# Seven half products for two up-projection tiles in the MLPs of a four-layer encoder

## Chip, core and metric

The kernel runs on one core of a Trainium2 chip. The metric is device time in microseconds for one call, the median of several runs. Engines are called by their names in the profile: PE is TensorE (PEld its weight loads), DVE is VectorE, ACT is ScalarE, POOL is GpSimd, and SP is the engine whose queue issues the loads.

## What is computed

A hybrid encoder with 4 layers on 512 tokens of 1024 features, in fp32. Each layer has a mixer (retention in layers 0 and 3, a convolution in layer 1, gated linear attention in layer 2) and an MLP, both with a norm before and behind. The change concerns the MLPs, whose inner width is 4096:

```python
def sq_relu_mlp(u, w_up, w_down):
    return jnp.square(jax.nn.relu(u @ w_up)) @ w_down

for i in range(DEPTH):
    ...
    u = rmsnorm(h, norm_gains[i, 2])
    h = h + rmsnorm(sq_relu_mlp(u, mlp_w_up[i], mlp_w_down[i]), norm_gains[i, 3])
```

## The kernel before

Activations lie with features on partitions: `X` is 8 blocks of 128 features by 512 tokens. To keep fp32 accuracy every operand is cut into a high and a low part (`h` and `l` at the end of a name), and `mm3` (L394) makes each product of three matmuls, high x high, high x low and low x high (L397 to L399). A weight panel is 8 blocks of 128x128: what one output tile of 128 features by 512 tokens reads.

`Stream` (L94) brings the panels in. `prep` loads one into `wraw` (three buffers, L130), ScalarE writes the high part `whi` (L137), VectorE the low part `wlo` (L138). Both go into a ring of six slots (`ring`, L104), so a panel's cut waits until TensorE is done with the panel six places before. `next` keeps three panels ahead. `cut_early` (L147) does the same for panels of the convolution that follows layer 0, and writes both parts back to DRAM (L158), from where they are later loaded ready made.

`mlp` (L540 and on) has `FB` = 4 blocks. A block makes 8 up tiles (`proj`, 24 matmuls of 512 columns each) and then 8 down tiles, which read the block's 8 activations `act`. `up` evacuates a tile: relu times the token norm on VectorE (L561) into a scratch tile `tmp` (four of these), square on ScalarE (L562), then its high (L378) and low part (L385). `down` copies the result into `y` on ScalarE in block 0 (L246) and adds it on VectorE later (L251). Block 0 begins with `lead`, four tiles in halves while the norm is still computed; the last four down tiles of block 3 go through `trail`, in halves of 256 columns. `step`, called after tiles, cuts an early panel at every second call.

The order on TensorE is that of the program. On the other engines a scheduler orders the instructions when the kernel is built; at run time each engine takes them strictly in that order, each waiting for its semaphores.

`first_norm` (L434) loads the input and the first panels at the start, and adds the squares of the input for the first norm between them, in an order of its own.

## Time and profile before

| | us |
|---|---|
| median of 3 runs | 2757.65 (2756.64 to 2759.5) |
| profiled execution | 2759.13 |
| its span, first to last instruction | 2757.4 |
| TensorE busy | 2694.0 (98%) |
| VectorE busy | 1635.7 (59%) |
| ScalarE busy | 1191.1 (43%) |

The span is cut into stages that follow each other on TensorE. A busy share of the whole span says little of one stage, so the stretches of the MLP are read on their own. "Idle before" in a group is the time its engine stood still right ahead of these instructions. The granted clock (PEclk) is a share of full speed.

### The profile page before, as it was taken

Reading aid. Unit: us, or ns where it says so; the run is one execution under the profiler, and the core shown is the slowest. Engines: PE = TensorE matmul, PEld = TensorE weight load, DVE = VectorE, ACT = ScalarE, POOL = GpSimd, SP = SyncE. Lnnn points to the kernel's source line nnn. Section 1 sums busy time; section 2 is a strip of 40 time slices with the busy share of each in tenths; the row PEclk is TensorE's granted clock in tenths of the full one; section 3 lists DMA queues with packets and bytes.
Section 4 is the critical chain, followed back from the end, with each engine's and each line's share of the span. In section 5 each row is a group of like instructions: output and inputs, shape, how many; then the busy total and the mean of one; then the engine's idle time right before and its main releaser. Section 6 shows DMA issues by size and latency. Waiting matters only on the chain.

```text
span 2757.4 us, 33473 instructions
## 1 busy us (share of the span) xinstructions
PE 2694.0 (98%) x13312; PEld 2281.1 (83%) x13312; DVE 1635.7 (59%) x2517; ACT 1191.1 (43%) x1801; POOL 136.5 (5%) x133
## 2 busy tenths in 40 slices
PE   9999999999999699999999999999999999999998
PEld 7788888788898498888887888888888888988887
DVE  7755568445459974444587684444665555844444
ACT  5442445434337554332377554333444443543322
POOL 4000000000008500000000000000000000000000
PEclk9999999999999899999999999999999999999999
DMA  4222132666544013223122222223112212132221
GB/s 175 70 76 100 69 107 100 250 238 239 210 159 171 16 32 115 96 96 102 67 70 73 73 100 99 92 99 128 66 67 92 84 69 98 56 115 94 98 102 44
DMA packets 82669, 289.98 MB, mean 105 GB/s; under 512 B 9168, under 2 KB 11472, under 8 KB 82512
## 3 DMA queue, kind: packets, MB, share of 16 engines
q1 hardware_dynamic: 82368, 287.77, 29.8%
q8 instruction: 104, 1.70, 0.3%
q14 instruction: 53, 0.43, 0.1%
q10 hardware_dynamic: 144, 0.07, 0.0%
HBM read 260.02 MB, written 27.79 MB: 104 GB/s over the span
## 4 chain that ended last, share of the span: by engine, by line
PE 85%; DVE 7%; POOL 3%; ACT 2%; DMA 1%; issue 1%; SPq 0%; DVEq 0%; POOLq 0%; ACTq 0%
PE ps L398 28%; PE ps L399 28%; PE ps L397 28%; POOL y L918 2%; DMA wraw<-in_wst_dram 1%; DVE ps L933 1%; DVE wlo L138 1%; DVE acc L210 1%; DVE tmp L272 0%; PE st L218 0%; DVE h L275 0%; ACT whi L137 0%; POOL f L619 0%; DVE actl L385 0%; POOL k L618 0%
## 5 line engine op out<-in xcount | busy, mean ns | idle before, releaser
L137 ACT ACTIVATE whi<-wraw 128x1024 fp32r<-128x1024 f32 (+1 forms) x396 | 414.5, 1050 | 818.2 <-PE ps L398 730.9
L397 PE MATMUL ps<-xh,whi 128*128 128x512 f32 (+1 forms) x1984 | 736.9, 371 | 3.5 <-DVE tmp L561 2.5
L398 PE MATMUL ps<-xl,whi 128*128 128x512 f32 (+1 forms) x1984 | 734.1, 370 | 1.1 <-DVE xl L387 1.1
L399 PE MATMUL ps<-xh,wlo 128*128 128x512 f32 (+1 forms) x1984 | 733.9, 370 | 0.0
L138 DVE TENSOR_TENSOR wlo<-wraw,whi 128x1024 fp32r<-128x1024 f32 (+1 forms) x396 | 482.4, 1221 | 219.8 <-ACT whi L137 218.4
L397 PEld LDWEIGHTS ps<-xh,whi 128*128 128x128 f32 x1984 | 374.4, 189 | 68.0 <-issue 3.4
L398 PEld LDWEIGHTS ps<-xl,whi 128*128 128x128 f32 x1984 | 374.4, 189 | 65.6 <-DVE xl L387 1.5
L399 PEld LDWEIGHTS ps<-xh,wlo 128*128 128x128 f32 x1984 | 374.2, 189 | 63.7 <-DVE wlo L138 0.4
L398 PE MATMUL ps<-actl,whi 128*128 128x512 f32 x896 | 349.8, 390 | 1.4 <-DVE actl L385 1.4
L397 PE MATMUL ps<-acth,whi 128*128 128x512 f32 x896 | 348.8, 389 | 1.8 <-ACT acth L378 1.8
L399 PE MATMUL ps<-acth,wlo 128*128 128x512 f32 x896 | 348.6, 389 | 0.0
L251 DVE TENSOR_TENSOR y<-y,ps 128x512 f32<-128x512 f32 (+1 forms) x200 | 114.6, 578 | 315.9 <-PE ps L399 315.4
L561 DVE SCALAR_TENSOR_TENSOR tmp<-ps,rx 128x512 f32<-128x512 f32 x128 | 86.8, 689 | 228.0 <-PE ps L399 227.7
L398 PEld LDWEIGHTS ps<-actl,whi 128*128 128x128 f32 x896 | 168.2, 188 | 40.6 <-DVE actl L385 5.9
L397 PEld LDWEIGHTS ps<-acth,whi 128*128 128x128 f32 x896 | 168.2, 188 | 37.2 <-ACT acth L378 2.2
L399 PEld LDWEIGHTS ps<-acth,wlo 128*128 128x128 f32 x896 | 168.2, 188 | 34.2
L210 DVE TENSOR_TENSOR acc<-acc,sq 128x256 f32<-128x256 f32 (+1 forms) x245 | 116.4, 479 | 50.9 <-ACT sq L209 45.0
L397 PE MATMUL ps<-whi,xh 128*128 128x512 f32 (+1 forms) x384 | 138.3, 360 | 1.3 <-ACT xh L380 1.1
L399 PE MATMUL ps<-whi,xl 128*128 128x512 f32 (+1 forms) x384 | 137.2, 357 | 0.0
L398 PE MATMUL ps<-wlo,xh 128*128 128x512 f32 (+1 forms) x384 | 137.0, 357 | 0.1
L209 ACT ACTIVATE sq<-y 128x256 f32<-128x256 f32 (+1 forms) x105 | 47.0, 455 | 127.2 <-DVE y L251 105.1
L385 DVE TENSOR_TENSOR actl<-tmp,acth 128x512 fp32r<-128x512 f32 x128 | 87.5, 689 | 4.1 <-ACT acth L378 4.0
(323 smaller groups left out, 3839.5 us busy)
## 6 DMA issues: line engine op xcount, KB each, us to landing
wraw<-in_wst_dram SPq DMA_DIRECT2D x438, 512.0 KB, 3.5
cuth<-early SPq DMA_DIRECT2D x24, 512.0 KB, 2.6
cutl<-early SPq DMA_DIRECT2D x24, 512.0 KB, 3.0
whi<-cuth SPq DMA_DIRECT2D x20, 512.0 KB, 3.3
wlo<-cutl SPq DMA_DIRECT2D x20, 512.0 KB, 4.2
h<-in_xT_dram SPq DMA_DIRECT2D x8, 256.0 KB, 5.4
wraw<-in_wst_dram SPq DMA_DIRECT2D x8, 256.0 KB, 5.3
ww<-cuth SPq DMA_DIRECT2D x4, 512.0 KB, 7.1
```

The lines of the kernel that those rows point to most:

```text
L137: nc.scalar.activation(h, raw[:, c:d], AF.Copy)
L138: nc.vector.tensor_tensor(l, raw[:, c:d], h.bitcast(F32), ALU.subtract)
L209: nc.scalar.activation(t, src, AF.Square, scale=scale)
L210: nc.vector.tensor_tensor(acc, acc, t, ALU.add)
L251: self.K.nc.vector.tensor_tensor(y, y, ps[:, a:b], ALU.add)
L385: self.nc.vector.tensor_tensor(lo, src, hi, ALU.subtract)
L397: mm(out, lhsT=A[0], rhs=B[0], start=start, stop=False)
L398: mm(out, lhsT=A[0], rhs=B[1], start=False, stop=False)
L399: mm(out, lhsT=A[1], rhs=B[0], start=False, stop=stop)
L561: nc.vector.scalar_tensor_tensor(t[:, lo:hi], ps[:, lo:hi], 0.0, self.r[:, lo:hi], ALU.max, ALU.mult)
L918: nc.gpsimd.tensor_tensor(co[i], co[i], o, ALU.add)
L933: nc.vector.scalar_tensor_tensor(sums[i], x, w, sums[i], ALU.mult, ALU.add)
```

## The change

In blocks 1 to 3 of every MLP, two neighbouring up tiles are computed together by Strassen's scheme in its form with seven products. The 2x2 parts are: two output tiles, two halves of the features (4 blocks each), two halves of the tokens (256 columns). Each of the seven products has 4 blocks and 256 columns.

The weights need sums of the raw parts. `Stream.pair` loads two panels and makes four entries of the ring from them: the first panel as it is, a sum panel `t`, a second sum panel, and a half panel. The sums are four VectorE instructions of 128x512 per pair. The operand sums of the activations (`combos`, with tiles `wS`) are made once per MLP, between the down tiles 2 to 5 of block 0. `seven` runs the products into three PSUM tiles, two of which are accumulated on: ScalarE copies the state between products into scratch tiles `e1` and `e2`, VectorE joins them, and the joined tile goes to the old evacuation `up` from SBUF in place of PSUM. It keeps five entries ahead.

The first two down tiles of each block run side by side (`proj2`): blocks 0 to 5 of the one, of the other, then blocks 6 and 7 of both. Early panels are cut after each down tile alone, into slots of the ring, no longer after up tiles and into tiles of their own. The squares for the first norm aren't added in `first_norm` any more but by `norm_sums`, called from `norm`. The diff, cut to its core:

```diff
 class Stream:
...
-    def cut_early(self, i, pool):
+    def pair(self, i):
...
+        pool = self.pairs.pop(i)
+        self.loaded += 2
+        H = 4 * P
+        r1 = pool.tile([P, 8 * P], F32, name="raw1", tag="raw1", bufs=2)
+        r2 = K.wp.tile([P, 8 * P], F32, name="wraw", tag="wraw", bufs=3)
+        nc.sync.dma_start(r1, self.src[i])
+        nc.sync.dma_start(r2, self.src[i + 1])
+        tt = nc.vector.tensor_tensor
+
+        def cut(raw, w=8 * P):
+            hi, lo = self.ring()
+            self.ready.append(Panel(hi, lo))
+            nc.scalar.activation(hi[0][:, :w], raw[:, :w], AF.Copy)
+            tt(lo[0][:, :w], raw[:, :w], hi[0][:, :w].bitcast(F32), ALU.subtract)
+
+        def second():
+            t = K.wp.tile([P, 8 * P], F32, name="wraw", tag="wraw", bufs=3)
+            tt(t[:, :H], r2[:, :H], r1[:, :H], ALU.subtract)
+            tt(t[:, H:], t[:, :H], r2[:, H:], ALU.subtract)
+            cut(t)
+
+            tt(r1[:, :H], r2[:, H:], r2[:, :H], ALU.subtract)
+            tt(r2[:, :H], t[:, H:], r1[:, H:], ALU.add)
+
+        cut(r1)
+        self.steps = [second, lambda: cut(r2), lambda: cut(r1, H)]
+
+    def cut_early(self, i):
...
-        hi, lo = (pool.tile([P, 8 * P], F32R, name="early", tag="early", bufs=2) for _ in range(2))
+        hi, lo = (t[0] for t in self.ring())
...
 def first_norm(self):
...
-        self.hsum = Sums(self, D)
...
-                if k:
-                    for a, b in HALVES:
-                        self.hsum.add(self.h[k - 1][:, a:b], (a, b))
-            for a, b in HALVES:
-                self.hsum.add(self.h[KD - 1][:, a:b], (a, b))
...
+    def proj2(self, X, late=2):
+
+        ps = [self.ps() for _ in range(2)]
+        p = []
+        for ks in (range(KD - late), range(KD - late, KD)):
+            for i in range(2):
+                if len(p) < 2:
+                    p.append(self.W.next())
+                for k in ks:
+                    self.mm3(ps[i], p[i].blk(k), X[k], k == 0, k == KD - 1)
+        return ps
...
+    def combos(self, pool):
...
+        def make(k):
+            xa, xb, s = self.tmp(), self.tmp(), self.tmp()
+            nc.scalar.activation(xa, self.h[k], AF.Identity, scale=self.gain(*self.X_gain, k))
+            nc.scalar.activation(xb, self.h[4 + k], AF.Identity, scale=self.gain(*self.X_gain, 4 + k))
+            tt(s[:, :H], xa[:, H:], xb[:, H:], ALU.add)
+            tt(s[:, H:], xa[:, :H], s[:, :H], ALU.subtract)
+            tt(xb[:, :H], xb[:, :H], s[:, H:], ALU.add)
+            tt(xb[:, H:], xa[:, :H], xa[:, H:], ALU.subtract)
+            c = (k % 2 * T, (k % 2 + 1) * T)
+            self.split(S12[k // 2], s, c)
+            self.split(S34[k // 2], xb, c)
...
+    def seven(self, evac):
...
+        a, c, bd = self.ps(), self.ps(), self.ps()
+        e1, e2 = self.tmp(), self.tmp()
+        lo, hi = slice(0, H), slice(H, T)
+
+        def product(n, out, w, off, more=False):
+            S = self.S[n]
+            for k in range(4):
+                self.mm3(out, w.blk(off + k), S[k], k == 0 and not more, k == 3, more)
...
+        w = entry()
+        product(1, a[:, lo], w, 0)
+        copy(e1[:, lo], a[:, lo])
+        product(2, bd[:, lo], w, 4)
+        w = entry()
+        product(5, c[:, lo], w, 0)
+        copy(e2[:, hi], c[:, lo])
+        product(6, a[:, lo], w, 4, True)
+        copy(e2[:, lo], a[:, lo])
+        w = entry()
+        product(4, bd[:, hi], w, 0)
+        product(3, c[:, lo], w, 4, True)
+        nc.vector.tensor_tensor(e2[:, lo], c[:, lo], e2[:, lo], ALU.add)
+        w = entry()
+        product(7, a[:, lo], w, 0, True)
+        copy(e1[:, hi], a[:, lo])
+        nc.vector.tensor_tensor(e2[:, hi], e1[:, hi], e2[:, hi], ALU.add)
+        evac(1, e2)
+        nc.vector.tensor_tensor(e1, bd, e1, ALU.add)
+        evac(0, e1)
+        W.at += 2
...
 def mlp(self, close, early=()):
...
-            steps += 1
-            if early and steps % 2 == 0:
-                self.W.cut_early(early.pop(0), mp)
+            if early:
+                self.W.cut_early(early.pop(0))
...
+                if b:
+                    for n in range(0, KD, 2):
+                        self.seven(lambda i, t: up(n + i, t, (0, T), t))
+                    n0 = KD
                 for n in range(n0, KD):
                     ps = self.proj()
                     self.when(lambda n=n, ps=ps: up(n, ps, (0, T)))
-                    step()
...
+                for n, ps in enumerate(self.proj2(act)):
+                    complete(n, ps)
+                for n in range(2, n1):
+                    complete(n, self.proj(act))
+                    if b == 0 and n < 6:
+                        make(n - 2)
```

**VectorE in an up-projection** (block 1 of layer 1; `tmp` scratch, `rx` the token norm). Before, an evacuation, a panel's low part, a low part of the activation, in turn:

```order
L561 SCALAR_TENSOR_TENSOR tmp_9482<-ps_9457,rx_8993 128x512
L138 TENSOR_TENSOR wlo_9561<-wraw_9559,whi_9560 128x1024
L385 TENSOR_TENSOR actl_9368<-tmp_9482,acth_9367 128x512
L561 SCALAR_TENSOR_TENSOR tmp_9518<-ps_9493,rx_8993 128x512
L138 TENSOR_TENSOR wlo_9597<-wraw_9595,whi_9596 128x1024
L385 TENSOR_TENSOR actl_9370<-tmp_9518,acth_9369 128x512
```

Now, from the join in the second pair (L657) to the cut of the last entry of the fourth (L176); L184 and L185 are sums of raw weights, L661 and L663 joins:

```order
L657 TENSOR_TENSOR tmp_10331<-ps_10328,tmp_10331 128x256
L176 TENSOR_TENSOR wlo_10430<-raw1_10425,whi_10429 128x1024
L427 TENSOR_TENSOR actl_10171<-tmp_10189,acth_10170 128x512
L176 TENSOR_TENSOR wlo_10465<-wraw_10461,whi_10464 128x1024
L184 TENSOR_TENSOR raw1_10425<-wraw_10426 128x512
L661 TENSOR_TENSOR tmp_10331<-tmp_10330,tmp_10331 128x256
L185 TENSOR_TENSOR wraw_10426<-wraw_10461,raw1_10425 128x512
L690 SCALAR_TENSOR_TENSOR tmp_10331<-tmp_10331,rx_9745 128x512
L663 TENSOR_TENSOR tmp_10330<-ps_10329,tmp_10330 128x512
L176 TENSOR_TENSOR wlo_10496<-wraw_10426,whi_10495 128x1024
L690 SCALAR_TENSOR_TENSOR tmp_10330<-tmp_10330,rx_9745 128x512
L176 TENSOR_TENSOR wlo_10526<-raw1_10425,whi_10525 128x512
```

Three instructions for a tile have become twelve for a pair, without those of the raw sums that stand further ahead.

**SP's queue in layer 0's down-projections** (`cuth`, `cutl` the DRAM copies of an early panel's parts; `wraw` loads by L130/L139 are panels, by L152/L195 early ones). Before, block 1:

```order
L130 DMA wraw_4637<-in_wst_dram 128x1024
L152 DMA wraw_4673<-in_wst_dram 128x1024
L158 DMA cuth137_4679<-early_4675 128x1024
L158 DMA cutl137_4680<-early_4676 128x1024
L130 DMA wraw_4683<-in_wst_dram 128x1024
L130 DMA wraw_4715<-in_wst_dram 128x1024
```

Now, block 0:

```order
L139 DMA wraw_4165<-in_wst_dram 128x1024
L195 DMA wraw_4198<-in_wst_dram 128x1024
L201 DMA cuth130_4148<-whi_4144 128x1024
L201 DMA cutl130_4149<-wlo_4145 128x1024
L139 DMA wraw_4221<-in_wst_dram 128x1024
L195 DMA wraw_4254<-in_wst_dram 128x1024
L201 DMA cuth131_4204<-whi_4200 128x1024
L201 DMA cutl131_4205<-wlo_4201 128x1024
```

Two panels were loaded for each early one; now each panel's load is followed by an early one with its two writes.

**VectorE at the start** (`acc` the sum of squares, `sq` its low part for the norm's matmul, which TensorE waits for). Before:

```order
L210 TENSOR_TENSOR acc<-acc,sq 128x256 x2
L138 TENSOR_TENSOR wlo<-wraw,whi 128x1024
L603 TENSOR_TENSOR alo<-ang,ahi 128x512
L758 TENSOR_SCALAR nlb<-lg 128x4
L764 TENSOR_SCALAR E<-dist,lg 128x896
L138 TENSOR_TENSOR wlo<-wraw,whi 128x1024
L385 TENSOR_TENSOR sq<-acc,sq 128x512
L765 SCALAR_TENSOR_TENSOR E<-dist,nlb,E 128x896
L138 TENSOR_TENSOR wlo<-wraw,whi 128x1024 x3
```

Now:

```order
L252 TENSOR_TENSOR acc<-acc,sq 128x256
L905 SCALAR_TENSOR_TENSOR E<-dist,nlb,E 128x896
L147 TENSOR_TENSOR wlo<-wraw,whi 128x1024
L252 TENSOR_TENSOR acc<-acc,sq 128x256
L147 TENSOR_TENSOR wlo<-wraw,whi 128x1024
L252 TENSOR_TENSOR acc<-acc,sq 128x256
L147 TENSOR_TENSOR wlo<-wraw,whi 128x1024
L252 TENSOR_TENSOR acc<-acc,sq 128x256
L427 TENSOR_TENSOR sq<-acc,sq 128x512
L147 TENSOR_TENSOR wlo<-wraw,whi 128x1024
```

The additions and `sq` have moved behind the fifth full panel; they stood behind the third.

## Rows read from the trace of the kernel before

**Rows 1.** The page, part 1: busy us (share of the span) x instructions

```profile
PE 2694.0 (98%) x13312; PEld 2281.1 (83%) x13312; DVE 1635.7 (59%) x2517; ACT 1191.1 (43%) x1801; POOL 136.5 (5%) x133
```

**Rows 2.** The waits, TensorE: line, releaser: us in total, times, longest us

```profile
PE ps L218 <- DVE acc L212: 16.3, 1, 16.3
...
PE ps L397 <- ACT acth L378: 1.8, 1, 1.8
PE ps L398 <- DVE actl L385: 1.4, 5, 0.4
```

**Rows 3.** The groups by form, TensorE: busy us, mean ns | idle, releaser

```profile
L397 PE MATMUL ps<-xh,whi 128*128 128x512 f32 x1616 | 631.6, 391 | 2.5 <-DVE tmp L561 2.5
...
L397 PE MATMUL ps<-xh,whi 128*128 128x256 f32 x368 | 105.3, 286 | 0.9 <-ACT xh L380 0.9
```

**Rows 4.** The timeline, TensorE, an up-projection and a trail: start us, us, instruction

```profile
537.44 0.39 PE L399 MATMUL ps<-xh,wlo 128*128 128x512 f32 x1
...
542.88 0.39 PE L399 MATMUL ps<-xh,wlo 128*128 128x512 f32 x1
...
772.38 0.28 PE L398 MATMUL ps<-actl,ww 128*128 128x256 f32 x1
...
779.34 0.28 PE L399 MATMUL ps<-acth,ww 128*128 128x256 f32 x1
```

**Rows 5.** The windows, ups, downs: us, busy PE, PEld, DVE, ACT, POOL; PEclk, DMA share, GB/s

```profile
539.00:582.00 43.00, 43.00 (x191) 35.60 (x190) 24.45 (x28) 21.00 (x29) 0.00 (x0) 1.00 0.66 240
582.00:625.50 43.50, 43.50 (x194) 36.02 (x193) 19.84 (x20) 12.27 (x13) 0.00 (x0) 1.00 0.67 241
```

**Rows 6.** The groups by form, VectorE

```profile
L138 DVE TENSOR_TENSOR wlo<-wraw,whi 128x1024 fp32r<-128x1024 f32 x388 | 476.9, 1232 | 219.0 <-ACT whi L137 217.6
L385 DVE TENSOR_TENSOR actl<-tmp,acth 128x512 fp32r<-128x512 f32 x128 | 87.5, 689 | 4.1 <-ACT acth L378 4.0
...
L251 DVE TENSOR_TENSOR y<-y,ps 128x512 f32<-128x512 f32 x120 | 82.1, 686 | 279.5 <-PE ps L399 279.4
...
L275 DVE TENSOR_TENSOR h<-h,tmp 128x256 f32<-128x256 f32 x128 | 53.2, 417 | 0.0
...
L138 DVE TENSOR_TENSOR wlo<-wraw,whi 128x512 fp32r<-128x512 f32 x8 | 5.5, 684 | 0.8 <-ACT whi L137 0.8
```

**Rows 7.** The timeline, VectorE, the first MLP: full stretches

```profile
477.77 2.48 DVE L561 SCALAR_TENSOR_TENSOR tmp<-ps,rx 128x512 f32<-128x512 f32 x4
...
664.93 1.23 DVE L155 TENSOR_TENSOR early<-wraw,early 128x1024 fp32r<-128x1024 f32 x1 [0.57 <-ACT early L154]
666.07 1.22 DVE L138 TENSOR_TENSOR wlo<-wraw,whi 128x1024 fp32r<-128x1024 f32 x1
```

**Rows 8.** The groups by form, ScalarE

```profile
L137 ACT ACTIVATE whi<-wraw 128x1024 fp32r<-128x1024 f32 x388 | 409.5, 1059 | 817.3 <-PE ps L398 730.9 <-DMA wraw<-in_wst_dram 31.8 <-PE ps L399 29.7
L378 ACT ACTIVATE acth<-tmp 128x512 fp32r<-128x512 f32 x128 | 79.6, 629 | 3.1
...
L380 ACT ACTIVATE vh<-ps,rcol 128x256 fp32r<-128x256 f32 x12 | 4.9, 470 | 6.9 <-PE ps L399 6.2 <-DVE rcol L1072 0.6
```

**Rows 9.** The timelines, TensorE and ScalarE, first down tile of layer 0

```profile
493.53 0.50 PE L397 MATMUL ps<-acth,whi 128*128 128x512 f32 x1 [1.78 <-ACT acth L378]
...
491.24 1.06 ACT L154 ACTIVATE early<-wraw 128x1024 fp32r<-128x1024 f32 x1 [1.17 <-DMA wraw<-in_wst_dram]
```

**Rows 10.** The windows, layer 0, stretches of 2 us in the downs, columns as in rows 5

```profile
590.00:592.00 2.00, 2.00 (x10) 1.66 (x9) 1.16 (x2) 0.00 (x0) 0.00 (x0) 1.00 1.05 406
592.00:594.00 2.00, 2.00 (x11) 1.65 (x10) 0.87 (x2) 1.06 (x1) 0.00 (x0) 1.00 1.00 311
```

**Rows 11.** The timelines at the start, TensorE, VectorE and ScalarE

```profile
31.66 0.62 PE L228 MATMUL st<-sq,onesr 128*128 128x512 f32 x2
...
27.47 0.68 DVE L385 TENSOR_TENSOR sq<-acc,sq 128x512 fp32r<-128x512 f32 x1
...
29.10 1.06 ACT L137 ACTIVATE whi<-wraw 128x1024 fp32r<-128x1024 f32 x1 [1.28 <-DMA wraw<-in_wst_dram]
```

More of the change, by code (lines that the diff above doesn't have):

```diff
@@ L114, in prep @@
         i = self.loaded
+        if i in self.pairs:
+            self.pair(i)
+            return []
         self.loaded += 1
@@ L161, in next @@
         ahead = self.ahead if ahead is None else ahead
-        while len(self.ready) < 1 + ahead and self.loaded < self.n:
-            self.prep()
+        self.fill(1 + ahead)
         self.at += 1
@@ L172, in fill @@
     def fill(self, n):
-        while len(self.ready) < n and self.loaded < self.n:
+        while len(self.ready) < n and (self.steps or self.loaded < self.n):
             self.prep()
@@ L537, in trail, with part @@
             self.after(5.0 if c[1] == T else 2.5, lambda c=c: close.half(c))
+    def combos(self, pool):
+        nc = self.nc
+        tt = nc.vector.tensor_tensor
+        H = T // 2
+        new = lambda: [pool.tile([P, 8 * P], F32R, name="wS", tag="w", bufs=8) for _ in range(2)]
+        S12, S34 = [new(), new()], [new(), new()]
+        def make(k):
[9 more added lines that the diff above has]
+            self.split(S34[k // 2], xb, c)
+        def part(S, which):
+            out = []
+            for k in range(4):
+                a = k % 2 * T + which * H
+                out.append(self.cut(S[k // 2], (a, a + H)))
+            return out
+        low, high = (0, H), (H, T)
+        self.S = {
+            1: [self.cut(self.X[k], low) for k in range(4)],
+            2: [self.cut(self.X[4 + k], low) for k in range(4)],
+            4: [self.cut(self.X[4 + k], high) for k in range(4)],
+            5: part(S12, 0), 6: part(S12, 1), 3: part(S34, 0), 7: part(S34, 1),
+        }
+        return make
```

36 lines of the change are left out of this document (27 added, 9 removed).

## Prediction

> **What bounds the kernel now.** The busy times come first: TensorE is busy for 2694.0 of 2757.4 us [rows 1]. Then its waits: the longest is one of 16.3 us inside the convolution, and the waits for the MLP's activations come to 1.8 and 1.4 us over the whole run [rows 2]. In an up-projection and in the down-projection behind it TensorE has no gap, at full clock, while VectorE is busy for 24.45 of 43.00 us and 19.84 of 43.50, and ScalarE for 21.00 and 12.27 [rows 5]. So in the MLPs the end is set by how fast TensorE issues, and a matmul that is gone is time that is gone, as long as the two engines that prepare its operands keep up.
>
> The duration of one matmul, 391 ns for 512 columns and 286 ns for 256 [rows 3], isn't its price, since they overlap. The price is the distance between starts. In an up-projection 24 matmuls of 512 columns take 542.88 - 537.44 = 5.44 us, 226.7 ns each; in the last part of a down-projection, where each has 256 columns and a weight load of its own, 58 take 779.34 - 772.38 = 6.96 us, 120.0 ns each [rows 4]. Two halves thus cost 13 ns more than one whole.
>
> **Fewer columns on TensorE.** A pair of up-projection tiles had 2 x 8 x 3 = 48 matmuls of 512 columns: 48 x 226.7 ns = 10.88 us. It gets seven products of 4 blocks x 3 matmuls with 256 columns: 84 x 120.0 ns = 10.08 us. That is 0.80 us a pair. Blocks 1 to 3 of four MLPs have 4 pairs each, 48 pairs: **38.4 us less**, if nothing waits. One block's up-projection goes from 43.5 to 40.3 us. The price of a 256-column matmul is the trace's; the only thing it doesn't show is the order of operands, and that is the same (a fresh weight block for each matmul, whole blocks of 128 columns).
>
> The Trainium skill would give more: "TensorE: Matmul & The Clock Gate", section "Back-to-back issue gap", puts the distance at N/2.4 + 2.5 ns, 109.2 ns for 256 columns and 215.8 for 512. By it a pair would save 48 x 215.8 - 84 x 109.2 = 1186 ns, and 48 pairs an estimated 57 us. The trace doesn't agree, with 120.0 and 226.7 ns: a fixed part of 13 ns per matmul instead of 2.5, and that part is what more and shorter matmuls multiply.
>
> **What VectorE and ScalarE get for it.** Weights for a pair were two panels, each cut into a high part on ScalarE (1059 ns) and a low part on VectorE (1232 ns). Now they are three panels and a half, plus four additions of 128x512 between raw panels. Results are put together from four copies on ScalarE and three additions on VectorE (two of 256 columns, one of 512) before the two old evacuations. VectorE per pair, by durations [rows 6]: 3 x 1232 + 684 for the cuts, 4 x 684 for the raw sums (taken as the 512-wide subtraction), 2 x 417 + 686 for the joins, 2 x 689 + 2 x 689 for the evacuations: 11.4 us, after 5.2 before. Its instructions overlap, though: in a full stretch starts lie 1.14 us apart for 1024 columns, and four of 512 take 2.48 us, 0.62 each [rows 7]. With these, and 0.35 for 256, the sum is 3 x 1.14 + 10 x 0.62 + 2 x 0.35 = 10.3 us. TensorE's pair takes 10.08. ScalarE per pair: 3 x 1059 + half of that for the half panel, 4 x 470 (bounded by the 256-column read of PSUM), 4 x 629 [rows 8]: 8.1 us. So VectorE is just as long as TensorE within a pair, and is the engine to watch.
>
> It isn't over the edge for a block, since work slips out at both ends. Weights are prepared into a ring of six: all of the first pair (7.1 us by durations) and the first panel of the second (1.2) can be cut during the down-projection before, where VectorE is less than half busy [rows 5]. The last pair's evacuation, about 3.9 us, falls into the down-projection behind. Two down panels (2.5 us) come in. Four pairs by durations: 45.5 - 8.3 - 3.9 + 2.5 = 35.8 us, in 40.3. In the order of VectorE's instructions the 12 between the second pair's join and the third's come to 9.3 us by durations and 8.4 by starts, under 10.08; and the weights for the third and fourth pairs stand some 8 us ahead of the matmuls that read them.
>
> The tightest place is the scratch tiles: there are four, two to a pair, so the first copy of the fourth pair waits for the second pair's last evacuation. From the end of the third pair's sixth product VectorE has to do a join, a low part, two down panels, a join and a low part: 0.42 + 0.69 + 2 x 1.23 + 0.42 + 0.69 = 4.7 us, then ScalarE's copy 0.47. TensorE comes to the product that needs it four products later, 4 x 1.44 = 5.8 us. That leaves 0.6 us for four hand-offs between engines. Behind the waiting copy stand ScalarE's cuts of the next panels. No wait of this kind is in the trace; between 0 and 2.5 us a block, I take **0.3 us x 12 = +3.6 us**, near zero, since sums by starts leave over a microsecond.
>
> **Side by side.** The first two down tiles now leave blocks 6 and 7 of the activations for last, 36 matmuls (8.2 us) after the start instead of 18 (4.1). The fourth pair's evacuation ends later than a tile's did (two tiles at once: a copy 0.47, two joins 0.42 and 0.69, two evacuations 0.69 each, a square and a high part 0.63 each, a low part 0.69, 4.9 us behind the last product), so this is what covers it; without it each block would wait up to 1 us. Of the 3.2 us of waits for activations it can take between 0 and all. The longest stands in layer 0, where the activation is queued on ScalarE behind an early panel whose load landed late [rows 9]; those early panels leave the up-projections altogether. **-2.5 us.** The operand sums (four steps of four 256-wide additions and two low parts, 3.0 us of VectorE each) lie in the first block's down-projection, where that block's results are copied by ScalarE and VectorE has under half its time in use: nothing.
>
> **Layer 0's early panels.** 24 panels for the convolution are cut and written to DRAM; they were spread over every second tile of ups and downs, and now go one to each down tile of blocks 0 to 2. On SP's queue, per tile of 5.44 us, stand two reads of 512 KB and two writes of 512 KB: 2.1 MB, 386 GB/s. With all 16 engines busy the trace shows 406 GB/s in a stretch with such writes and 311 in the reads behind it [rows 10], so a tile needs about 1.05/0.311 + 1.05/0.406 = 6.0 us of transfers. Over eight tiles some 4 us are missing, three times. Panels are two tiles ahead, which hides that; what is left over shifts the start of the next up-projection's preparation, with VectorE nearly full. Between 0 and 12 us, **+3 us**, since the lead of the ring is longer than the lag. The early panels also take ring slots, so the first pair has only its first three entries ready there.
>
> **The start.** The sums of squares for the first norm were added in a fixed order among the first panels; now the scheduler puts them later. Their result was ready by 27.47 + 0.68 us, and TensorE read it at 31.66 [rows 11]. Now it stands on VectorE behind the fifth full panel, whose high part starts at 29.10: about 29.10 + 1.06 + 1.23, then an addition 0.42, a high part 0.63 and a low part 0.68 [rows 6, 8]: 33.1. **+1.5 us**, between 0 and 3.
>
> **Sum.** -38.4 + 3.6 - 2.5 + 3 + 1.5 = -32.8 us. The profiled execution took 2759.13 us with a span of 2757.4; the median of the runs is 2757.65, 1.5 lower. The change, summed on the profiled execution, is taken off the median: 2757.65 - 32.8 = 2724.9, say **2725 us**. With each of these costs at its best: 2757.65 - 38.4 - 3.2 = 2716.
>
> **Rivals.** (1) Hand-offs between ScalarE and VectorE cost more than 0.3 us a block. For it: VectorE has 10.3 to 11.4 us of work in a pair of 10.08, strictly in order, and each low part waits for a high part, which waits for a ring slot. Against: the 35.8 us of 40.3. At 1.5 to 2.3 us a block, 14 to 24 us more than I took: 2739 to 2749. (2) Layer 0's transfers aren't hidden: 12 us for the missing bandwidth, 9 more than I took, and as much again if the writes, which wait for both cuts, hold the reads behind them on SP: 2734 to 2746. (3) The other side: VectorE can't work ahead, because its queue stands at a join or a low part that waits for a ring slot until the up-projection begins. Then all 45.5 + 2.5 = 48.0 us lie in each of 12 up-projections of 43.5: +4.5 x 12 = 54 us, and with the other terms 2757.65 + 54 - 2.5 + 4.5 = 2814. It decides from 3.2 us of waits a block on, where the matmuls' gain is used up. (4) Waits of just that size: within 0.2% of before.
>
> **How the numbers follow.** A measurement of this kernel tells 0.2%, 5.5 us, from no change. My forecast, 2716 to 2735, has 0.62; rival 1 0.18; rival 2 beyond 2735 0.08; rival 4 0.05; rival 3 0.07. Faster: 0.62 + 0.18 + 0.08 = 0.88; same 0.05; slower 0.07. The range takes in the forecast and the first two rivals: 2714 to 2749.
>
> **What would show it.** In an up-projection after: starts of 256-column matmuls 0.12 us apart and pairs of 10.1 us; blocks of 40.3 to 40.8 us from the first product to the first down matmul; TensorE's waits for scratch copies and evacuations below 6 us in sum; VectorE busy for over 85% of the up-projections. Layer 0's downs should show transfers near full share and 43.5 us all the same. If starts are further apart than 0.12 us, the first term is wrong; if pairs are 10.5 us or longer with TensorE waiting on ScalarE's copies, rival 1 holds; if the waits are on low parts of weights, it is rival 3, or rival 2 where layer 0 alone has them.

## The result, and the profile after

The changed kernel takes **2717.48 us** (median of 4 runs, 2715.87 to 2719.07), the kernel before 2757.14 us beside it (4 runs, 2755.18 to 2759.5). The ratio is 0.9856, interval 0.9839 to 0.9873: 39.7 us faster. The prediction was 2725, range 2714 to 2749. Sign and size are right, but several terms of its sum are not, and one of them by far.

The profiled execution took 2716.43 us with a span of 2714.7, which is 42.7 us under the span of before. That is 3 us more than the medians say, because before's profiled run is late in its range and after's early. Part 1 of the page, and the waits of TensorE that are new or changed:

```profile
PE 2655.4 (98%) x15040; PEld 2332.1 (86%) x15040; DVE 1937.0 (71%) x3045; ACT 1363.1 (50%) x2153; POOL 135.2 (5%) x133
```

```profile
PE ps L440 <- DVE actl L427: 3.5, 8, 1.1
...
PE ps L439 <- ACT tmp L639: 1.3, 2, 1.0
...
PE st L270 <- ACT sq L420: 1.0, 1, 1.0
```

TensorE runs 1728 more matmuls in 39 us less busy time [rows 1]. The waits that the prediction feared (copies of the products, L639) occur twice in the whole run, and no low part of a pair's weights is waited for. The timeline of TensorE in an up-projection of layer 1, and three windows (columns as in rows 5): layer 0's block 1 ups, layer 1's block 1 ups, and the downs behind the latter. The last line is the kernel before, layer 1's block 1 ups:

```profile
1087.65 0.28 PE L439 MATMUL ps<-xh,whi 128*128 128x256 f32 x1
...
1088.85 0.28 PE L440 MATMUL ps<-xl,whi 128*128 128x256 f32 x1
```

```profile
521.90:564.00 42.10, 40.76 (x337) 40.34 (x336) 37.71 (x53) 28.00 (x46) 0.00 (x0) 1.00 0.56 186
1087.70:1128.00 40.30, 40.30 (x338) 40.30 (x337) 33.05 (x46) 27.08 (x44) 0.00 (x0) 1.00 0.43 136
1128.00:1171.50 43.50, 43.50 (x194) 36.01 (x193) 23.92 (x30) 10.87 (x13) 0.00 (x0) 1.00 0.22 69
```

```profile
1102.40:1145.80 43.40, 43.40 (x193) 35.95 (x192) 19.22 (x22) 17.00 (x23) 0.00 (x0) 1.00 0.28 97
```

Ten matmuls lie 1.20 us apart, the 0.120 us of [rows 4]. TensorE has no gap in 40.30 us, while VectorE is busy for 33.05 of them: 82%, in the same block before 44% (19.22 of 43.40; the windows of [rows 5] are from layer 0, where early panels are cut too). Only layer 0's ups differ.

Cut by the starts of the first matmul of each stage in TensorE's timeline, the 42.7 us of the spans come from here:

| stage | before | after | difference |
|---|---|---|---|
| start of the program to the first projection behind the scores | 121.9 | 118.6 | -3.3 |
| layer 0, block 0: second half of the ups, downs | 27.18, 47.14 | 22.28, 44.34 | -7.7 |
| ups of blocks 1 to 3, 11 of 12 | 43.52 each | 40.31 each | -35.3 |
| the twelfth, block 1 of layer 0 | 43.52 | 42.15 | -1.4 |
| layer 0, downs of blocks 1 to 3 (3: its first half) | 43.52, 43.52, 21.76 | 44.77, 44.98, 22.19 | +3.1 |
| first half of the downs of block 3, layers 1 and 2 | 21.76, 21.76 | 22.69, 22.42 | +1.6 |
| all else | | | +0.2 |

So the scheme gives 36.7 us in the ups. The other 6 are a balance of gains and losses around it, which the experiments take apart. In "all else" +1.0 in the convolution of layer 1 and -0.7 in layer 2's mixer stand against each other; both stages vary by that much among the kernels shown here.

### The profile page after: what moved, and what is told of

Its sections match the earlier page's. It is cut to its first block, busy times and chain, and to the rows that moved or that the text cites. A ratio compares the mean times of both kernels' runs of the same rounds, so it can differ in the third digit from the quotient of the medians.

```text
span 2714.7 us, 38029 instructions
## 1 busy us (share of the span) xinstructions
PE 2655.4 (98%) x15040; PEld 2332.1 (86%) x15040; DVE 1937.0 (71%) x3045; ACT 1363.1 (50%) x2153; POOL 135.2 (5%) x133
## 4 chain that ended last, share of the span: by engine, by line
PE 83%; DVE 8%; ACT 3%; DMA 2%; POOL 2%; issue 1%; SPq 0%; DVEq 0%; POOLq 0%; ACTq 0%
PE ps L440 27%; PE ps L441 27%; PE ps L439 27%; POOL y L1058 2%; DVE wlo L147 1%; DVE ps L1073 1%; DMA wraw<-in_wst_dram 1%; DVE acc L252 1%; DMA cuth<-whi 1%; DMA cutl<-wlo 1%; DVE tmp L314 1%; ACT whi L146 0%; DVE actl L427 0%; DVE h L317 0%; PE st L260 0%
## 5 line engine op out<-in xcount | busy, mean ns | idle before, releaser
L439 PE MATMUL ps<-xh,whi 128*128 128x256 f32 (+1 forms) x1792 | 600.3, 335 | 0.9 <-ACT xh L422 0.9
L440 PE MATMUL ps<-xl,whi 128*128 128x256 f32 (+1 forms) x1792 | 597.7, 334 | 1.1 <-DVE xl L429 1.1
L441 PE MATMUL ps<-xh,wlo 128*128 128x256 f32 (+1 forms) x1792 | 597.3, 333 | 0.0
L146 ACT ACTIVATE whi<-wraw 128x1024 fp32r<-128x1024 f32 (+1 forms) x300 | 312.2, 1045 | 315.5 <-PE ps L440 212.8
L147 DVE TENSOR_TENSOR wlo<-wraw,whi 128x1024 fp32r<-128x1024 f32 (+1 forms) x300 | 365.6, 1222 | 109.3 <-ACT whi L146 108.0
L439 PEld LDWEIGHTS ps<-xh,whi 128*128 128x128 f32 x1792 | 340.3, 190 | 35.3 <-ACT xh L422 1.1
L439 PE MATMUL ps<-wS,whi 128*128 128x256 f32 x768 | 217.5, 283 | 1.3 <-ACT tmp L639 1.3
L440 PE MATMUL ps<-wS,whi 128*128 128x256 f32 x768 | 217.3, 283 | 0.0
L441 PE MATMUL ps<-wS,wlo 128*128 128x256 f32 x768 | 217.3, 283 | 0.0
L175 ACT ACTIVATE whi<-wraw 128x1024 fp32r<-128x1024 f32 x96 | 101.5, 1057 | 144.5 <-PE ps L440 111.2
L175 ACT ACTIVATE whi<-raw 128x1024 fp32r<-128x1024 f32 x96 | 81.2, 846 | 160.0 <-PE ps L440 128.2
L439 PEld LDWEIGHTS ps<-wS,whi 128*128 128x128 f32 x768 | 147.4, 192 | 1.7 <-ACT tmp L639 1.7
```

The source lines that it names most:

```text
L146: nc.scalar.activation(h, raw[:, c:d], AF.Copy)
L147: nc.vector.tensor_tensor(l, raw[:, c:d], h.bitcast(F32), ALU.subtract)
L175: nc.scalar.activation(hi[0][:, :w], raw[:, :w], AF.Copy)
L439: mm(out, lhsT=A[0], rhs=B[0], start=start, stop=False)
L440: mm(out, lhsT=A[0], rhs=B[1], start=False, stop=False)
L441: mm(out, lhsT=A[1], rhs=B[0], start=False, stop=stop)
```

## The experiments

Each ran beside the kernel before; those named a_ are edits of the changed kernel, those named b_ of the kernel before. Where one number is given it is a single profiled run.

**a_no_side: without the two tiles side by side**

```diff
-                for n, ps in enumerate(self.proj2(act)):
-                    complete(n, ps)
-                for n in range(2, n1):
+                for n in range(n1):
                     complete(n, self.proj(act))
-                    if b == 0 and n < 6:
+                    if b == 0 and 2 <= n < 6:
```

> The changed kernel with the first two down tiles one after the other again. My prediction gave the side-by-side order a worth of up to 1 us a block: by that the time rises by at most 12 us, to 2717-2730 us. The trace of the changed kernel says more: in layer 1, block 1, the last low part of the activations ends 6.85 us behind the last product, and a single tile reads it from 4.1 us on, so 2 to 3 us a block in blocks 1 to 3, and as much again where a wait that long lowers the clock: 2740 to 2760 us, nearly all of the gain. Told apart by the waits of TensorE for acth and actl at the first down tiles: under 12 us in sum, or over 25.

Measured: 2787.4 us, beyond what was expected, before 2759.21; ratio 1.0099, interval 1.0082 to 1.0116. It is **slower than before** by 28 us, and 70 us behind the changed kernel. The ups still take 40.31 us; the downs of layer 1 take 45.6, 47.9 and 46.2 and 29.1 in the half block, where after has 44.3, 43.5, 43.5 and 22.7. Of the 70 us, 26 lie in layer 0. Its waits, then TensorE's timeline and windows at the first down tile of block 1, layer 1:

```profile
PE ps L439 <- ACT acth L420: 35.1, 16, 4.1
...
PE ps L440 <- DVE actl L427: 10.2, 19, 2.1
```

```profile
1161.34 0.50 PE L439 MATMUL ps<-acth,whi 128*128 128x512 f32 x1 [1.90 <-ACT acth L420]
1162.07 0.50 PE L440 MATMUL ps<-actl,whi 128*128 128x512 f32 x1 [0.23 <-DVE actl L427]
...
1164.16 0.63 PE L441 MATMUL ps<-acth,wlo 128*128 128x512 f32 x1
1164.59 0.63 PE L439 MATMUL ps<-acth,whi 128*128 128x512 f32 x1
```

```profile
1161.00:1163.00 2.00, 1.43 (x5) 0.98 (x6) 0.69 (x1) 0.29 (x1) 0.00 (x0) 1.00 0.07 29
1163.00:1165.00 2.00, 2.00 (x7) 1.55 (x6) 1.29 (x2) 1.06 (x1) 0.00 (x0) 0.59 0.00 0
1165.00:1167.00 2.00, 2.00 (x7) 1.55 (x6) 1.93 (x3) 0.00 (x0) 0.00 (x0) 0.56 0.00 0
```

This stage loses 4.35 us (47.87 - 43.52) by waits of 2.13. Behind the wait come matmuls 0.43 us apart in place of 0.227, at a granted clock of 0.59 and 0.56 in these windows, which is the lower of the two levels (1.2 GHz) for most of them. One block later the same wait is not followed by this:

```profile
1249.52 0.50 PE L439 MATMUL ps<-acth,whi 128*128 128x512 f32 x1 [1.90 <-ACT acth L420]
```

```profile
1251.00:1253.00 2.00, 2.00 (x10) 1.65 (x9) 1.13 (x2) 1.06 (x1) 0.00 (x0) 1.00 0.00 0
```

The clock stays at 1.00, and that stage loses 2.69 us (46.21). So the fall of the clock is worth 1.7 of the 4.35 us. Of the six stages of blocks 1 and 2 in layers 1 to 3, which all have these waits, the other five lose 4.1 to 4.35 us. Waits of 45 us for activations, where after has 3.5, cost 70 in all.

**b_side: the same side-by-side order in the kernel before, without pairs** (the rows of `proj2` and `complete` from the change, nothing else)

> The kernel before with the first two down tiles of each block side by side and nothing else. Waits for activations come to 3.2 us in the kernel before, most of it 1.78 us in layer 0, with 3 us of matmuls at the lower clock behind it. Theory (side by side is worth its 70 us with the pairs only, whose last evacuation ends some 6 to 7 us behind the last product): gain of 0 to 4 us here, 2753 to 2757, downs of 43.5 us as before outside layer 0. Rival (it helps by itself, in each of 16 blocks): downs shorter by 0.3 us or more each, 5 us or more in sum.

Measured: 2758.02 us, before 2757.26, one run each. Every down-projection outside block 0 takes 43.52 us, as before. In layer 0's block 0 the downs take 44.58 us in place of 47.14, and the wait of 1.78 us for `acth` [rows 9] is gone. (I was wrong to expect a lower clock behind that wait: in before the matmuls after 493.53 us lie 0.227 us apart.) These 2.6 us don't show in the whole run, where the runs of before alone spread over 4 us. So the same order is worth under 3 us in the kernel before and 70 in the changed one; the gains of the two parts of the change don't add.

**b_early: in the kernel before, early panels after down tiles alone, in slots of the ring**

```diff
-        hi, lo = (pool.tile([P, 8 * P], F32R, name="early", tag="early", bufs=2) for _ in range(2))
+        hi, lo = (t[0] for t in self.ring())
...
-            steps += 1
-            if early and steps % 2 == 0:
+            if early:
...
                     self.when(lambda n=n, ps=ps: up(n, ps, (0, T)))
-                    step()
```

> The kernel before with one part of the change alone: layer 0's early panels cut after down tiles only, into slots of the ring. Theory: they are what shortened layer 0's block 0 (ups from 27.2 to 22.3 us, downs from 47.1 to 44.3), so both shorten here as well, by 6 to 8 us together, and the later downs of layer 0 lengthen by 1 to 2 us each; sum -3 to -6 us. Rival: these 7.7 us came from the side-by-side tiles and from elsewhere in the MLP; then layer 0's block 0 stays at 27 and 47 us and the time is that of before or a few us above it.

Measured: 2756.09 us, before 2759.21. The second half of block 0's ups takes 22.28 us in place of 27.18, exactly as in after. What stood there, in the kernel before (timeline, then windows):

```profile
478.61 0.47 PE L397 MATMUL ps<-xh,whi 128*128 128x512 f32 x1 [2.53 <-DVE tmp L561]
```

```profile
479.00:481.00 2.00, 2.00 (x7) 1.55 (x6) 2.00 (x4) 1.64 (x4) 0.00 (x0) 0.52 0.58 234
481.00:483.00 2.00, 2.00 (x7) 1.60 (x6) 2.00 (x3) 2.00 (x4) 0.00 (x0) 0.62 0.28 115
```

A wait for an evacuation, and behind it the lower clock again. And the down-projection of block 1 in this kernel, with one early panel to each tile, as one window:

```profile
571.00:614.50 43.50, 43.50 (x194) 36.02 (x193) 23.56 (x24) 16.29 (x17) 0.00 (x0) 1.00 0.94 323
```

The transfers fill 0.94 of the engines' time, at 323 GB/s, and TensorE has no gap. So the bandwidth that the prediction found missing costs nothing in blocks 1 and 2, where no pairs follow. Block 0's downs got longer, 48.98 for 47.14, against the expectation, and the later downs didn't.

**a_skip: no early panel after the last down tile of a block**

```diff
-                    step()
+                    if n < KD - 1:
+                        step()
```

> The changed kernel without the early panel that was cut after the last down tile of a block in layer 0 (7, 7, 7 and 3 panels in the four blocks, in place of 8, 8 and 8). Theory: layer 0 loses 5.0 us in after because a ring slot is still being written to DRAM when ScalarE comes to it at the start of an up-projection, and the copies of the products stand behind it in ScalarE's order; with nothing written there, block 1's ups go from 42.15 to 40.3 us and the downs of blocks 1 and 2 from 44.8 and 45.0 to 44.4 or less: 3 to 5 us less, 2712 to 2715. Rival (the missing bandwidth of the transfers): the same 24 panels have to be moved, so 0 to 1.5 us, 2716 to 2718, with the waits moved to block 3.

The reason to try it is this pair of rows of after, at the start of block 1's ups in layer 0 (timelines, ScalarE and TensorE):

```profile
524.60 1.06 ACT L175 ACTIVATE whi<-raw 128x1024 fp32r<-128x1024 f32 x1 [2.44 <-DMA cuth<-whi]
525.57 1.04 ACT L175 ACTIVATE whi<-wraw 128x1024 fp32r<-128x1024 f32 x1
526.51 0.58 ACT L288 ACTIVATE y<-ps 128x512 f32<-128x512 f32 x1
526.99 0.37 ACT L639 ACTIVATE tmp<-ps 128x256 f32<-128x256 f32 x1
```

```profile
527.41 0.39 PE L439 MATMUL ps<-wS,whi 128*128 128x256 f32 x1 [1.03 <-ACT tmp L639]
```

ScalarE stands for 2.44 us at a ring slot whose early panel is still being written to DRAM. The first copy of a product has to wait behind it in ScalarE's order, and TensorE waits for that copy. Measured: block 1's ups go to 40.31 us, as the theory said. But the downs of blocks 1 and 2 stay at 45.0 and 45.1, and the run at 2717.15 us (ratio 0.9853, interval 0.9838 to 0.9868): the same as the changed kernel, and short of the theory's 3 to 5 us. Nor does the early panel alone make the loss in the ups: a_sums, below, keeps it, ScalarE stands for 2.34 us at the same place, and block 1's ups take 40.41 us; there the write lands 1.7 us earlier in the stage. (Block 3's ups take 41.49 in a_sums.) In a_skip's profiled run the start took 3.2 us longer than in after's, 121.8 us to the first projection, with a wait of 4.4 us for `sq`. VectorE's instructions stand in the same order there, and some took longer, like this one, the same in both (timelines of VectorE, a_skip, then after):

```profile
31.81 1.48 DVE L252 TENSOR_TENSOR acc<-acc,sq 128x256 f32<-128x256 f32 x1
```

```profile
29.40 0.83 DVE L252 TENSOR_TENSOR acc<-acc,sq 128x256 f32<-128x256 f32 x1
```

Both additions lie in a stretch in which POOL computes too; before POOL begins, at 20.8 us, an addition of this form takes 0.42 us in both runs. Apart from the start, a_skip's span is 0.3 us under that of after: the start varies by far more than this edit is worth.

**a_three: three down tiles side by side, and a_skip_three: that and no early panel after the last tile**

```diff
-    def proj2(self, X, late=2):
+    def proj2(self, X, late=2, side=3):
-        ps = [self.ps() for _ in range(2)]
+        ps = [self.ps() for _ in range(side)]
...
-                for n in range(2, n1):
+                for n in range(3, n1):
...
-                    if b == 0 and n < 6:
-                        make(n - 2)
+                    if b == 0 and n < 7:
+                        make(n - 3)
```

> The changed kernel with three down tiles side by side in place of two, which puts 54 matmuls (12.2 us) ahead of the first that reads block 6 of the activations. Theory: two tiles (8.2 us) cover the last pair's evacuation, 6 to 7 us, except at the end of blocks 0 (44.33 us, 0.8 over 43.52) and of block 3 in layers 1 and 2 (0.9 and 0.7 over); the three tiles take away up to 0.8 x 4 + 1.6, nothing in layer 0's later blocks, where ScalarE's wait is the cause: 1 to 5 us less, 2712 to 2716. Rival (the third PSUM tile held so long delays evacuations): 0 to 5 us more.

> Both. If the two causes are separate, their gains add up: 4 to 10 us less than the changed kernel, 2708 to 2713. If both act on the same wait, no more than the larger of the two.

Measured: 2724.61 us (ratio 0.9875, interval 0.9858 to 0.9891) and 2720.09 (0.9862, 0.9847 to 0.9877). Both expectations missed, in layer 0 alone. In layers 1 to 3 the half downs of block 3 are back at 21.79 us (-1.6 in sum), and layer 0's downs of blocks 1 and 2 at 43.55 in a_three. But layer 0's ups grow. In a_three they take 44.4, 44.7 and 45.2, by a wait that after doesn't have. In a_skip_three those of blocks 2 and 3 take 44.2 and 42.7, by another one: TensorE waits for a copy of a product (2.25 us at 612.87), and ScalarE comes late to that copy, after standing at an early panel whose load was late (a_three's waits, then ScalarE's timeline in a_skip_three):

```profile
PE ps L441 <- DVE wlo L176: 6.3, 3, 2.2
```

```profile
609.08 1.06 ACT L197 ACTIVATE whi<-wraw 128x1024 fp32r<-128x1024 f32 x1 [6.17 <-DMA wraw<-in_wst_dram]
```

As I read it (not tried apart), the down panels of three tiles and the early panels hold ring slots for longer, and what is loaded behind them comes late. Block 0's 44.33 us didn't move either: my expectation had put them to the pair's evacuation, and block 0 has no pairs.

**a_best: three tiles side by side in layers 1 to 3 alone; early panels skip block 0's last tile and the first of blocks 1 to 3**

```diff
+        side = 2 if early else 3
...
-                    step()
+                    if n != (0 if b else KD - 1):
+                        step()
```

> The changed kernel with three down tiles side by side in layers 1 to 3 and two in layer 0; in layer 0 no early panel is cut after block 0's last down tile nor after the first of blocks 1 to 3 (7, 7, 7 and 3 panels). In the order of VectorE the second early panel of a block then stands behind the last low part of the activations, where it stood ahead of it. Theory: the 5.0 us that layer 0 loses in after are VectorE and ScalarE standing at ring slots that are still written to DRAM, with the activations (downs of blocks 1 and 2, 1.3 and 1.5 us) or the copies of the products (ups of block 1, 1.8 us) behind them in order; so block 1's ups go to 40.3 us, the downs of blocks 1 and 2 to 43.6, and block 3's downs of layers 1 and 2 lose 1.6 us: 4.5 to 6.5 us less than the changed kernel with an equal start, 2711 to 2714. Rival (bandwidth, or a wait that goes elsewhere in layer 0): only the 1.6 us and part of the 5.0, 2715 to 2718.

Measured: **2714.46 us** (2713.93 to 2716.38, 5 runs; before 2758.18), ratio 0.9843, interval 0.9830 to 0.9857. Block 1's ups in layer 0 take 40.31 us and block 3's half downs in layers 1 and 2 take 21.8, as expected. The downs of blocks 1 and 2 don't follow, at 45.39 and 45.12, so that of the 4.5 to 6.5 us expected 3.0 came between the medians and 2.0 between the profiled spans. The early panel is out of the way, but the next instruction meets the same thing (VectorE's timeline after block 1's ups, layer 0; the last line is from after):

```profile
569.11 0.69 DVE L427 TENSOR_TENSOR actl<-tmp,acth 128x512 fp32r<-128x512 f32 x1 [1.72 <-ACT acth L420]
570.84 1.22 DVE L147 TENSOR_TENSOR wlo<-wraw,whi 128x1024 fp32r<-128x1024 f32 x1 [1.03 <-DMA cutl<-wlo]
571.98 0.68 DVE L427 TENSOR_TENSOR actl<-tmp,acth 128x512 fp32r<-128x512 f32 x1
```

```profile
571.68 1.23 DVE L198 TENSOR_TENSOR wlo<-wraw,whi 128x1024 fp32r<-128x1024 f32 x1 [1.20 <-DMA cutl<-wlo]
```

Now it is an ordinary panel's low part that waits at a slot under writing, with the last low part of the activations behind it; in after it was an early panel's (1.20 us). This fits the cause, but the cure for the downs fails. It is the fastest version here; its interval overlaps with that of the changed kernel, so that the 3 us between them are likely but not established.

**a_dup2 and a_dup4: one of the raw sums done three and five times** (the result is the same; the rows are a_dup2's, a_dup4 has `range(5)`)

```diff
-            tt(r1[:, :H], r2[:, H:], r2[:, :H], ALU.subtract)
+            for _ in range(3):
+                tt(r1[:, :H], r2[:, H:], r2[:, :H], ALU.subtract)
```

> The changed kernel with one of the four raw sums of each pair of up panels (512 columns, 0.62 us by starts) done three times instead of once: 1.24 us more of VectorE's time a pair, 5 us a block; the result stays the same. In the kernel after, VectorE is busy for 33.05 of 40.40 us in an up-projection. Theory (VectorE has room, the ring's lead carries it): 38.0 of 40.4 still fits, ups stay within 0.3 us of 40.31, the whole run at 2716 to 2722. Rival (VectorE strictly in order is already at its edge, hand-offs take what is added): each block grows by over half of the 5 us, 12 blocks by 30 us or more, 2745 or later.

> The same sum five times instead of once: 2.5 us more of VectorE's time a pair, 10 us a block. Theory (what decides is VectorE's sum over the block and what slips into the downs): 33 + 10 = 43 us in an up-projection of 40.3 is over the edge, part of it slips into the down-projection before and behind (23.9 of 43.5 busy), so ups of 41 to 43.5 us with waits of TensorE for low parts of weights or scratch copies; 12 blocks by 1 to 3 us, 2728 to 2755. If VectorE's free time in the downs were open to it in full, ups would stay at 40.3 and the run at 2717 to 2722. If it can't work ahead at all, ups reach 45 us and the run 2770 or more.

Measured: 2741.26 and 2813.41 us. With two more sums the ups of layers 1 to 3 still take 40.31 us each; the 25 us are lost elsewhere, in layer 0's ups (42.0, 43.0, 43.9) and the half downs of block 3 (29.1, 27.6, 26.3, 25.1). With four more they go to 45.0 and 46.1 us in layer 1. Windows of block 1 in layer 1, ups and downs of a_dup2, then the ups of a_dup4 and its waits:

```profile
1101.00:1141.30 40.30, 40.30 (x337) 40.29 (x336) 33.69 (x48) 25.09 (x42) 0.00 (x0) 1.00 0.34 114
1141.30:1184.80 43.50, 43.50 (x194) 36.03 (x193) 28.20 (x36) 12.77 (x15) 0.00 (x0) 1.00 0.30 90
```

```profile
1118.90:1163.90 45.00, 42.31 (x337) 41.89 (x336) 37.00 (x53) 25.32 (x42) 0.00 (x0) 0.96 0.30 95
```

```profile
PE ps L440 <- ACT whi L175: 23.6, 13, 2.6
PE ps L440 <- ACT acth L421: 20.4, 10, 5.7
```

Of the 5 us added a block in a_dup2, VectorE does 0.6 in the up-projection (33.69 for 33.05) and 4.3 in the down-projection (28.20 for 23.92): it works ahead, or behind, as the prediction had it. Where the neighbouring stage has no room for that, the whole run pays at once: both theories for a_dup2 missed, and neither had the loss in block 3. With 10 us a block TensorE waits for weights (23.6 us for high parts, and 11.1 for low parts), and the time is beyond the main theory's 2755; the last case, ups of 45 us and 2770 or more, came, though VectorE is busy for 37.00 of 45.00 us. For the ups of layers 1 to 3 the edge lies between 1.2 and 2.5 us more of VectorE's time a pair. For the whole run it lies below 1.2.

**a_deep1: one entry ahead in place of five**

```diff
-        self.deep = 5
+        self.deep = 1
```

> The changed kernel with one entry of weights prepared ahead in the up-projections in place of five. Theory: the lead is what lets VectorE, with 10.3 us of work to a pair of 10.08, use the down-projection before; with one entry, 2.9 us ahead, most of its 45 us falls into each up-projection and TensorE waits for low parts of weights: 43 to 48 us an up-projection instead of 40.3, +30 to +90 us in all. Rival: the ring of six slots and the order of the scheduler give the lead anyway; then the up-projections stay below 41 us and the time within 5 us of the changed kernel.

Measured: 2716.49 us, ups of 40.31 us, as in after (42.57 in layer 0's block 1). The lead doesn't come from this number. What is left is the rival, the ring of six and the order of the scheduler; neither was varied.

**b_sums and a_sums: the sums of squares moved in the kernel before, and put back in the changed kernel**

```diff
         self.warm(14)
-        self.hsum = Sums(self, D)
...
-                if k:
-                    for a, b in HALVES:
-                        self.hsum.add(self.h[k - 1][:, a:b], (a, b))
```

(for b_sums, with the last addition behind them; a_sums is the reverse)

> The kernel before with the first norm's sums of squares taken out of the start's fixed order, nothing else. My prediction: +1.5 us. The traces: the first attention scores of layer 0 end 3.3 us earlier in the changed kernel. If the sums' place did that, this kernel shows the same 3.3 us by 120 us after the start, with the waits for qkl at 78 us down from 2.7 us to under 2 and no wait for rx; if the start differs for another reason, nothing or +1.5 us.

> The changed kernel with the squares for the first norm added where the kernel before added them, among the first panels. If the move of these sums gave the 3.3 us that the start gained (the first projection behind the scores begins at 118.6 us in after, 121.9 before), it begins at 120 to 122 us here and the run takes 2718 to 2720. If the start gained for another reason, it stays at 118.6 to 119, and the run at 2716 to 2717.

Measured: 2758.2 us for b_sums, with before at 2759.21, and 2721.7 for a_sums, a little over what was expected. The first projection behind the scores begins at 118.8 us in b_sums and at 122.5 in a_sums. Over all twelve kernels and after it begins at 120.3 to 122.5 us with the sums in their old place, before included, and at 118.5 to 119.4 with them moved, except in a_skip. So moving the sums gives about 3 us (1 to 4 between single runs), though TensorE does wait for `sq`. The wait of 2.0 us for the token norm `rx` in before (1.2 in a_sums) is gone with it. The rows of before, then of after, say where the rest is (timeline, windows):

```profile
81.88 0.50 PE L399 MATMUL ps<-qkh,qkl 128*128 128x512 f32 x1 [2.74 <-DVE qkl L385]
```

```profile
82.00:86.00 4.00, 4.00 (x12) 2.96 (x13) 3.27 (x5) 2.09 (x3) 0.00 (x0) 0.64 0.44 156
```

```profile
79.29 0.50 PE L441 MATMUL ps<-qkh,qkl 128*128 128x512 f32 x1 [0.91 <-DVE qkl L427]
81.03 0.50 PE L441 MATMUL ps<-qkh,qkl 128*128 128x512 f32 x1 [0.77 <-DVE qkl L427]
```

```profile
82.00:86.00 4.00, 4.00 (x19) 3.29 (x19) 3.90 (x7) 2.08 (x4) 0.00 (x0) 1.00 0.75 226
```

With the sums moved, one wait of 2.74 us becomes two short ones, and the lower clock behind it (0.64) is gone. (In b_early a wait of 2.39 us at this place was not followed by a lower clock, and its first projection begins earliest of those with the sums in the old place, at 120.3.) With the sums put back the wait is back (a_sums's waits):

```profile
PE ps L441 <- DVE qkl L427: 2.7, 1, 2.7
```

Which moved instruction lets `qkl` come earlier I didn't follow up. b_sums as a whole gains 1 us at most. Of the 3.1 us at its start, 0.4 go in block 0 of layer 0 (second half of the ups 28.83 for 27.18, downs 45.87 for 47.14) and 1.4 in the convolution of layer 1 with the tiles before it, which takes 0.8 to 2.3 us longer in every other kernel here than in the profiled run of before.

## Why the prediction was right, and where it wasn't

**Fewer columns: right.** 12 x (43.52 - 40.31) = 38.5 us, for 38.4. In 11 of the 12 blocks it came whole. The distance of 0.120 us from the trace carried over to the new operands. The 57 us that the prediction estimated from the Trainium skill ("TensorE: Matmul & The Clock Gate", section "Back-to-back issue gap") did not come. That section gives the formula for an isolated matmul, and puts matmuls of 512 columns in a stream with weight loads at about 131 ns each. The 226.7 ns of this trace agree with neither. Reading the price from the distance between starts, and not from durations, is what made this term.

**Hand-offs: +3.6 taken, nothing measured** outside layer 0. The tight place, 4.7 us against 5.8, holds, and the block's sum on VectorE (35.8 us estimated) is 33.05 to 34.23 in layer 1. "Over 85%" was therefore too high there (82 to 85%); in layer 0, with the early panels, it came (90 to 93%). Rivals 1 and 3 fall: TensorE doesn't wait in 11 of 12 blocks. a_dup2 shows that VectorE does move work into the down-projections, which rival 3 denied. It also shows that this was a near thing: 1.24 us more a pair cost 25 us. (The windows of [rows 5] begin 6 us late in their stages. Cut to the stages, VectorE is busy there for 23.60 us in the ups and 20.45 in the downs, which leaves the argument as it is.)

**Side by side: the step that failed.** The prediction took off 2.5 us, the waits of layer 0, and wrote that without it each block would wait up to 1 us. The 2.5 us came (b_side, and the next paragraph). The 1 us is wrong. In after, the last low part of block 1's activations in layer 1 starts at 1134.12 us (VectorE's timeline), 6.9 us by its end behind the last product at 1127.96, where I had summed 4.9. The timelines show what that sum left out, ScalarE's first, then VectorE's:

```profile
1128.05 1.06 ACT L146 ACTIVATE whi<-wraw 128x1024 fp32r<-128x1024 f32 x1 [0.38 <-PE ps L440]
1129.02 0.36 ACT L639 ACTIVATE tmp<-ps 128x256 f32<-128x256 f32 x1
```

```profile
1129.14 1.23 DVE L147 TENSOR_TENSOR wlo<-wraw,whi 128x1024 fp32r<-128x1024 f32 x1 [0.19 <-ACT whi L146]
1130.28 0.42 DVE L661 TENSOR_TENSOR tmp<-tmp 128x256 f32<-128x256 f32 x1
...
1134.12 0.69 DVE L427 TENSOR_TENSOR actl<-tmp,acth 128x512 fp32r<-128x512 f32 x1 [0.64 <-ACT acth L420]
```

A cut of a down panel stands in the way twice. The last copy waits behind a high part on ScalarE and starts 1.06 us after the last product, and the join waits behind the low part of the same panel on VectorE, for 0.9 us after the copy has ended. From the join to the end it takes 4.53 us, where the same steps were summed to 4.4: the steps were right, and what stood ahead of them in the two queues was left out. With 4.1 us of cover, in a_no_side, waits of 2.1 us follow in blocks 1 and 2 of layers 1 to 3 (more in block 3 and in layer 0), and mostly a lower clock behind them: 70 us. With 8.2 us of cover the blocks 1 and 2 of layers 1 to 3 show nothing of it. The forecast survived because the change itself has this cover; for the change without it the prediction's own steps would have given 2727 to 2740 (no relief, up to 1 us in 12 blocks), and 2787 is the answer.

**The relief in layer 0: -7.7 for -2.5.** These are two things. The 2.8 us in the downs of block 0 are the side-by-side order, which gives 2.6 there by itself in b_side: the prediction's 2.5, in place and about in size (one trace each; b_sums, which lacks this order, has 45.87 there). Its reason, that the early panels leave the up-projections, isn't what does it: b_early moves them alone, and these downs get longer. The other 4.9 us, in the ups, are the early panels' leaving, as b_early shows without the rest of the change. The prediction didn't have them: it missed the wait of 2.5 us for an evacuation, which stands in the first line of [rows 3], and the lower clock behind it.

**Layer 0's early panels: +3 taken, +5.0 measured** (1.83 in block 1's ups over 40.31; 1.25, 1.46 and 0.43 in the downs), by another mechanism. Rival 2's missing bandwidth falls: in b_early the downs of blocks 1 and 2, with the same early panels at 0.94 of the engines' time, take 43.52 us. Its other half, reads held up behind the writes on SP, isn't excluded; a_skip_three's late load would fit it. The rows of after show the loss at ring slots that a write still holds, with ScalarE and VectorE strictly in order behind them; the part in block 1's ups is gone in a_skip, and nearly gone in a_sums, where the write lands earlier, and a_best showed the part in the downs moving to the next instruction.

**The start: +1.5 taken, -3.3 measured.** The two waits for `sq` came as told, 1.0 and 0.5 us. What failed is the step after it: I didn't ask what else would stand elsewhere in VectorE's order when these additions moved, up to the scores 50 us later. The size is uncertain, since the start alone took 3.2 us longer in a_skip.

**Not foreseen:** +1.6 us in block 3, where cuts of the four panels for the last tiles stand between the last evacuations on ScalarE and VectorE; a_three and a_best remove it.

The sum: predicted -32.8 us, -42.7 in the profile. The differences are hand-offs -3.6, relief -5.2, start -4.8, early panels +2.0, block 3 +1.6: together -10.0. The errors mostly had one sign: a cost that didn't come, and waits that vanished with the lower clock behind them.

## What to carry to other kernels

A scheme that saves matmuls hands its bill to the evacuation. Count the time from the last product to the last operand as a chain across engines, with whatever stands ahead of each step in its engine's order, and give the next stage at least that much work that doesn't need it; without such cover the saving here turned into a loss. A wait of TensorE of some two microseconds costs about double where the granted clock falls behind it, as it did in five of six equal stages here. And a buffer shared with a transfer to DRAM stays taken until the write is done: what stands behind its next user in that engine's order is what the transfer really costs.

## What the runs showed of the hardware

Three waits of 1.9 to 2.7 us shown above (1161.34 us in a_no_side, 478.61 and 81.88 in before) were followed by 3 to 4 us of matmuls of 512 columns 0.43 us apart, in windows with a granted clock of 0.52 to 0.64, and then by full speed again. I had read the waits of before without looking at the stretch behind them. But the equal wait of 1.90 us at 1249.52 us in a_no_side, and that of 1.78 us at 493.53 in before, were followed by matmuls 0.227 us apart at a granted clock of 1.00. With the fall a stage lost 4.35 us, without it 2.69. These traces don't show what decides between the two. And the additions at the start, of 256 columns and in the same order in a_skip and in after, took 0.42 us before POOL began to compute, and 0.42 to 1.51 us beside it; one and the same addition took 1.48 us in the one and 0.83 in the other, and why isn't shown.
